# Three quarters of an MLP's down projection as seven block products instead of eight

## The chip, the cores and the metric

The kernel runs on one core of one Trainium2 chip, as one program. The metric is device time in microseconds, the median of several runs. The traces are single executions taken by the hardware profiler.

## The reference

Two post-norm residual layers over x of 512 tokens by 1024 features, in float32. Each layer has a token mixer (mLSTM in layer 0, causal pooling in layer 1), a four-head cross attention into 256 memory tokens whose keys and values both layers share, and an MLP. After each of the three, x becomes LayerNorm(alpha * x + sublayer(x)). The part that changes is the second product of this:

```python
def sq_relu_mlp(x, w1, b1, w2, b2):
    return jnp.square(jax.nn.relu(x @ w1 + b1)) @ w2 + b2
```

with w1 of 1024 x 4096 and w2 of 4096 x 1024 in each layer. Of the rest it matters that `mem_k` and `mem_v` are computed once and read by `memory_cross_attn` in layer 0 and again in layer 1.

## The kernel before

Each float32 operand of a large product is split into a high part h (rounded for TensorE's float32r) and a low part l, the remainder. `mm3` (L167) makes one tile product of three matmuls: h by h, h by l, l by h (L168, L169, L170). A weight unit of 128 x 1024 is loaded into `raw`, cast to `wh` by ScalarE (L131) and turned into `wl = raw - wh` by VectorE (L132); there are three `raw` buffers and five each of `wh` and `wl`, shared by all weights of the program.

The MLP goes by four quarters q of the 4096 hidden features (L733). In each, the **up** part makes eight tiles of 128 hidden features by 512 tokens (`feat_tile`, 24 matmuls of 512 columns each); `evh` (L711) turns a tile into the hi and lo parts of relu squared with two operations on ScalarE and two on VectorE. The **down** part (L721) goes by two halves of 512 output columns: four weight units, then for each of four groups of 128 tokens eight `mm3` into one PSUM bank (24 matmuls of 512 columns), and VectorE adds the bank onto x (L726). A down part is 2 x 4 x 24 = 192 matmuls. In layer 0 the last quarter also sets up and runs the pooling mixer of layer 1 (`pool_setup`, L560), by halves of the tokens, with up tiles of 256 columns. The keys and values of the memory lie in eight tiles of the pool `vkv` from before layer 0's attention until layer 1's attention.

The code names tiles and a scheduler decides the order: each engine gets one fixed list of instructions and works through it from the first to the last, and an instruction waits for semaphores of the other engines. All loads are issued by SyncE (SP) into one queue, in the order of its list. So an instruction that waits holds up everything behind it on its engine.

The lines that the prediction uses:

```python
        h = wh_p.tile([P, WU], F32R, tag="wh", name=f"wh{n}")
        l = wl_p.tile([P, WU], F32R, tag="wl", name=f"wl{n}")
        A.copy(h, r)
        V.tensor_tensor(l, r, f32(h), ALU.subtract)
```

```python
                ps = token_proj(f"m{n}{hf}{t}", hid, w, t)
                V.tensor_tensor(x[t][:, hs], x[t][:, hs], ps, ALU.add)
```

Of the kernel before, what the change touches and what calls it, by code (L numbers as in the profile page):

```python
# [15 lines left out]
P = 128  # L16
# [5 lines left out]
H = 4  # L22
# [19 lines left out]
def trunk(ctx: ExitStack, tc: tile.TileContext, a: dict, out: bass.AP):  # L42
# [29 lines left out]
    class Act:  # L72
        """hi and lo parts of a feature-major array [1024, S], in two halves of 512 features"""
# [15 lines left out]
    def t5(name, dt=F32):  # L89
        return t5_p.tile([P, 1280], dt, tag="t5", name=name)  # L90

    def t2(name, n=512, dt=F32):
        return t2_p.tile([P, 512], dt, tag="t2", name=name)[:, :n]

    class ActT:
        """hi and lo parts of a feature-major array [1024, S], in two halves of 256 tokens"""
# [161 lines left out]
    def feat_first(name, n, srcs, x, evac):  # L258
        """The first n tiles of 128 features, the first half of the tokens ahead of the second"""
# [38 lines left out]
    for q in range(4):  # L298
        r = vkv_p.tile([P, 2, 516], F32, tag="vkv", name=f"xr{q}")[:, :, :S]
# [40 lines left out]
    def scores(h):  # L340
        """(k q^T) * exp(log weights) of head h, hi and lo, by tiles of keys"""
# [33 lines left out]
    # v: token-major, with a column of ones for the denominator  # L375
    vh = [vkv_p.tile([P, NT, 258], F32R, tag="vkv", name=f"vh{h}") for h in range(H)]
    vl = [vkv_p.tile([P, NT, 258], F32R, tag="vkv", name=f"vl{h}") for h in range(H)]
# [74 lines left out]
    # o gate  # L452
# [51 lines left out]
    def mem_k(n):  # L504
        """K^T of heads 2n, 2n + 1"""
        t = [vkv_p.tile([P, 1032], F32R, tag="vkv", name=f"k{n}{p}")[:, :1024] for p in "hl"]
# [8 lines left out]
    def mem_v():  # L515
        for mt in range(2):
            mv.append([vkv_p.tile([P, 1032], F32R, tag="vkv", name=f"v{mt}{p}")[:, :1024] for p in "hl"])
# [101 lines left out]
    for i in range(DEPTH):  # L619
        # cross attention  # L620
# [112 lines left out]
        for q in range(4):  # L733
# [17 lines left out]
            first = 0  # L751
            if q == 0:
                feat_first(f"h{n}", 4, lambda m: a["w1"][i, m], xm, lambda c, ps: evh(hid.k(c), c, q, ps, n))
                first = 4
                assert not later
                b2 = t5(f"b2{i}")[:, :D]
                ld(b2, a["b2"][i : i + 1, :].broadcast_to([P, D]))
                for t in range(NT):
                    V.scalar_tensor_tensor(x[t], x[t], ALPHA, b2, ALU.mult, ALU.add)
            for m in range(first, KC):  # L760
                evh(hid.k(m), m, q, feat_tile(f"h{n}{m}", a["w1"][i, 8 * q + m], xm, aux_p, "aux"), n)
            for hf in range(2):
                for t in down(hid, q, hf, range(NT), n):
                    for z in range(2):
                        ld(out[tok(t), hf_cols(z)], x[t][:, hf_cols(z)])


def _layout(inp):
    c = np.ascontiguousarray

    def feat(w):
        """[D, n * 128] -> [n, 128 (of a k tile), k tile, 128]"""
# [3 lines left out]
    def half(w):  # L776
        """[D, n * 512] -> [n, 4, 128, 2 k tiles * 512]"""
# [69 lines left out]
```

## Time and profile before

| | |
|---|---|
| runs | 1244.35, 1247.54, 1248.63 us, median 1247.54 |
| span of the profiled execution | 1242.4 us |
| TensorE busy | 1231.8 us (99%), 6457 matmuls |
| VectorE busy | 711.6 us (57%) |
| ScalarE busy | 503.8 us (41%) |
| DMA | 139.85 MB, mean 113 GB/s |

The page gives no time for the profiled execution but its span; the median of the runs is 5.1 us above it. A busy share is an average over the whole span, so a stage has to be read by itself. A matmul's record is longer than its turn on the engine, since matmuls are pipelined: the distance from one start to the next is what one costs.

### The profile page before, as it was taken

Reading aid. Unit: us, or ns where it says so; the run is one execution under the profiler, and the core shown is the slowest. Engines: PE = TensorE matmul, PEld = TensorE weight load, DVE = VectorE, ACT = ScalarE, POOL = GpSimd, SP = SyncE. Lnnn points to the kernel's source line nnn. Section 1 sums busy time; section 2 is a strip of 40 time slices with the busy share of each in tenths; the row PEclk is TensorE's granted clock in tenths of the full one; section 3 lists DMA queues with packets and bytes.
Section 4 is the critical chain, followed back from the end, with each engine's and each line's share of the span. In section 5 each row is a group of like instructions: output and inputs, shape, how many; then the busy total and the mean of one; then the engine's idle time right before and its main releaser. Section 6 shows DMA issues by size and latency. Waiting matters only on the chain.

```text
span 1242.4 us, 16082 instructions
## 1 busy us (share of the span) xinstructions
PE 1231.8 (99%) x6457; PEld 1053.7 (85%) x6457; DVE 711.6 (57%) x1062; ACT 503.8 (41%) x773; POOL 8.5 (1%) x34
## 2 busy tenths in 40 slices
PE   9999999999999999999999999999999999999997
PEld 6877889889889888888889899998988888888886
DVE  6775466485559534425356889775853442534446
ACT  7576675334423513314235454552351331422420
POOL 0000000000000000000000000000000000000000
PEclk9999999999999999999999999999999999999999
DMA  6232346333323423323336545532332332422411
GB/s 236 64 102 85 103 137 217 119 107 106 98 85 90 131 85 102 102 68 120 118 109 196 169 131 161 170 100 68 103 119 85 107 97 68 131 73 88 133 51 68
DMA packets 41786, 139.85 MB, mean 113 GB/s; under 512 B 5068, under 2 KB 5324, under 8 KB 41712
## 3 DMA queue, kind: packets, MB, share of 16 engines
q1 hardware_dynamic: 41712, 138.84, 35.5%
q8 instruction: 50, 0.82, 0.3%
q14 instruction: 24, 0.20, 0.0%
HBM read 136.72 MB, written 2.10 MB: 112 GB/s over the span
## 4 chain that ended last, share of the span: by engine, by line
PE 94%; DVE 3%; DMA 2%; issue 1%; ACT 0%; SPq 0%; DVEq 0%; ACTq 0%
PE h L169 9%; PE h L168 9%; PE h L170 9%; PE m L170 9%; PE m L168 9%; PE m L169 9%; PE ao L169 2%; PE ao L170 2%; PE ao L168 2%; PE q L169 2%; PE q L170 2%; PE q L168 2%; PE v L168 1%; PE qk L170 1%; PE qk L168 1%; PE v L170 1%
## 5 line engine op out<-in xcount | busy, mean ns | idle before, releaser
L131 ACT CAST wh<-raw 128x1024 fp32r<-128x1024 f32 x232 | 244.3, 1055 | 540.3 <-PE m L170 217.0
L132 DVE TENSOR_TENSOR wl<-raw,wh 128x1024 fp32r<-128x1024 f32 x232 | 283.8, 1224 | 262.7 <-ACT wh L131 257.3
L726 DVE TENSOR_TENSOR xp<-xp,m 128x512 f32<-128x512 f32 x32 | 22.0, 686 | 82.3 <-PE m L170 82.3
L726 DVE TENSOR_TENSOR xin<-xin,m 128x512 f32<-128x512 f32 x32 | 21.9, 686 | 65.9 <-PE m L170 65.9
L168 PE MATMUL h<-xm01h,wh 128*128 128x256 f32 (+1 forms) x176 | 59.0, 335 | 0.0
L168 PE MATMUL h<-xm00h,wh 128*128 128x256 f32 (+1 forms) x176 | 58.5, 333 | 0.0
L170 PE MATMUL h<-xm00h,wl 128*128 128x256 f32 (+1 forms) x176 | 58.4, 332 | 0.0
L170 PE MATMUL h<-xm01h,wl 128*128 128x256 f32 (+1 forms) x176 | 58.3, 331 | 0.0
L169 PE MATMUL h<-xm00l,wh 128*128 128x256 f32 (+1 forms) x176 | 58.3, 331 | 0.0
L169 PE MATMUL h<-xm01l,wh 128*128 128x256 f32 (+1 forms) x176 | 58.3, 331 | 0.0
L168 PE MATMUL h<-xm10h,wh 128*128 128x512 f32 (+1 forms) x144 | 52.8, 367 | 0.0
L168 PE MATMUL h<-xm11h,wh 128*128 128x512 f32 (+1 forms) x144 | 52.8, 367 | 0.0
L169 PE MATMUL h<-xm10l,wh 128*128 128x512 f32 (+1 forms) x144 | 52.6, 366 | 0.0
L170 PE MATMUL h<-xm11h,wl 128*128 128x512 f32 (+1 forms) x144 | 52.6, 365 | 0.0
L170 PE MATMUL h<-xm10h,wl 128*128 128x512 f32 (+1 forms) x144 | 52.6, 365 | 0.0
L169 PE MATMUL h<-xm11l,wh 128*128 128x512 f32 (+1 forms) x144 | 52.6, 365 | 0.0
L714 ACT ACTIVATE r<-h,b 128x512 f32<-128x512 f32 (+1 forms) x72 | 45.6, 634 | 0.3 <-PE h L170 0.2
L716 DVE TENSOR_TENSOR s<-r 128x512 f32<-128x512 f32 (+1 forms) x72 | 45.0, 625 | 0.0
L169 PEld LDWEIGHTS h<-xm00l,wh 128*128 128x128 f32 x176 | 33.4, 190 | 3.2
L168 PEld LDWEIGHTS h<-xm00h,wh 128*128 128x128 f32 x176 | 33.4, 190 | 3.2
L170 PEld LDWEIGHTS h<-xm01h,wl 128*128 128x128 f32 x176 | 33.4, 190 | 3.2
L168 PEld LDWEIGHTS h<-xm01h,wh 128*128 128x128 f32 x176 | 33.4, 190 | 3.1
(594 smaller groups left out, 3268.4 us busy)
## 6 DMA issues: line engine op xcount, KB each, us to landing
raw<-in_w SPq DMA_DIRECT2D x144, 512.0 KB, 3.7
raw<-in_w_q SPq DMA_DIRECT2D x24, 512.0 KB, 4.4
raw<-in_w_ao SPq DMA_DIRECT2D x16, 512.0 KB, 3.7
raw<-in_w_qk SPq DMA_DIRECT2D x8, 512.0 KB, 4.5
raw<-in_w_v SPq DMA_DIRECT2D x8, 512.0 KB, 4.7
raw<-in_w_o SPq DMA_DIRECT2D x8, 512.0 KB, 4.2
raw<-in_w_k SPq DMA_DIRECT2D x8, 512.0 KB, 3.9
raw<-in_w_kvv SPq DMA_DIRECT2D x8, 512.0 KB, 4.7
```

The costliest lines, as they stand in the source:

```text
L131: A.copy(h, r)
L132: V.tensor_tensor(l, r, f32(h), ALU.subtract)
L168: T.matmul(out_, l[0], r[0], start=start, stop=False)
L169: T.matmul(out_, l[0], r[1], start=False, stop=False)
L170: T.matmul(out_, l[1], r[0], start=False, stop=stop)
L714: A.activation(r, ps, AF.Relu, bias=b1[:, i, 8 * q + c : 8 * q + c + 1], scale=1.0)
L716: V.tensor_tensor(s, r, r, ALU.mult)
L726: V.tensor_tensor(x[t][:, hs], x[t][:, hs], ps, ALU.add)
```

## The change

In the first three quarters of each layer's MLP, the down part takes the 512 tokens x 1024 hidden features as 2 x 2 blocks A11, A12, A21, A22 and the quarter of w2 as B11 to B22, and makes their product from seven block products. `product` (new) is one of them: two PSUM banks, each of four `mm3`, so 24 matmuls of 512 columns. The squared hidden tiles stay in float32 (`s`), and VectorE makes the sums of blocks; each of the seven left operands is split into hi and lo by a cast of 1024 columns on ScalarE and a subtraction of 1024 columns on VectorE (`split`), each of the seven right operands by two of each (`weight_split`), and the sums of weights are eight more additions of 1024 columns (`each`). Four products are gathered in SBUF over the quarters (`into`: a copy by ScalarE in the first quarter, an addition by VectorE in the others), three are added to x at once (`onto`), and after the third quarter `gather` adds the four gathered sums to x in sixteen operations of 512 columns.

The new tiles need room: the pools `vkv`, `t5` and `t2` become a scope that is closed while the three quarters run and opened again for the fourth. So the keys and values are written to DRAM during layer 0 and read back before the fourth quarter.

```diff
+        if i == 0:
+            kv_flat = [z for w in mk + mv for z in w]
+            spill = dram_p.tile([len(kv_flat), P, 1024], F32, name="spill")
+            for n, z in enumerate(kv_flat):
+                ld(spill[n], f32(z))
...
+        enter(hid=12, rawd=6, t2=2)
...
+        def product(name, lhs, rhs, evac):
+
+            for g in range(2):
+                ps = acc_p.tile([P, 512], F32, tag="acc", name=f"{name}{g}")
+                for k in range(4):
+                    w = rhs[k // 2]
+                    mm3(ps, tuple(z[:, k, tok(g)] for z in lhs), (w[0][:, k % 2], w[1][:, k % 2]), start=k == 0, stop=k == 3)
+                evac(g, ps)
...
+                A.activation(r, ps, AF.Relu, bias=b1[:, i, 8 * q + m : 8 * q + m + 1], scale=1.0)
+                A.activation(s[m // 4][:, m % 4], r, AF.Square)
...
+                if m == 3 or m == first == 4:
+                    L["M1"] = split(f"a11{n}", a11)
+                    V.tensor_tensor(a11, a11, a21, ALU.subtract)
+                    L["M7"] = split(f"q3{n}", a11)
+            V.tensor_tensor(a21, a21, a22, ALU.subtract)
+            L["M5"] = split(f"q1{n}", a21)
+            V.scalar_tensor_tensor(a11, a11, -1.0, a22, ALU.mult, ALU.subtract)
+            L["M6"] = split(f"q2{n}", a11)
+            L["M2"] = split(f"a12{n}", a12)
+            V.tensor_tensor(a12, a12, a11, ALU.add)
+            L["P3"] = split(f"q4{n}", a12)
+            L["P4"] = split(f"a22{n}", a22)
...
+            b11 = load("b11", 0, 0)
+            product(f"m1{n}", L["M1"], weight_split(f"b11{n}", b11), into("M1"))
+            b12, b22 = load("b12", 1, 0), load("b22", 1, 2)
+            each(b11, b11, b12, ALU.add)
+            each(b12, b12, b22, ALU.add)
+            product(f"m7{n}", L["M7"], weight_split(f"t3{n}", b12), into("M7"))
+            product(f"m5{n}", L["M5"], weight_split(f"t1{n}", b11), into("M5"))
+            each(b11, b11, b22, ALU.add)
+            product(f"m6{n}", L["M6"], weight_split(f"t2{n}", b11), into("M6"))
+            product(f"p3{n}", L["P3"], weight_split(f"b22{n}", b22), onto(0, 1))
+            b21 = load("b21", 0, 2)
+            product(f"m2{n}", L["M2"], weight_split(f"b21{n}", b21), onto(0, 0))
+            each(b11, b11, b21, ALU.add)
+            product(f"p4{n}", L["P4"], weight_split(f"t4{n}", b11), onto(1, 0))
...
+                V.tensor_tensor(u, u, m7, ALU.add)
+                V.tensor_tensor(x21, x21, u, ALU.add)
...
+        for q in range(3):
+            up_down(q, f"{i}{q}")
+        gather()
+        enter(**mixing)
+        if i == 0:
...
+            for n, z in enumerate(kv_flat):
+                ld(f32(z), spill[n])
```

On TensorE's list a down part now holds 7 x 24 = 168 matmuls, in the order M1, M7, M5, M6, P3, M2, P4. Three places of the other lists matter; a name is the program's, with the layer and the quarter at its end (`t201l0`: low part of the first unit of the sum of weights t2, layer 0, quarter 1).

**Place 1: VectorE (DVE) from the last up tile of layer 0's second quarter into its down part.** Before:

```order
L719 TENSOR_TENSOR h011l_4371<-s017_4516,h011h_4370 128x512
L726 TENSOR_TENSOR xin0_2110<-xin0_2110,m0100_4544 128x512
L726 TENSOR_TENSOR xin1_2112<-xin1_2112,m0101_4570 128x512
L726 TENSOR_TENSOR xin2_2114<-xin2_2114,m0102_4596 128x512
L132 TENSOR_TENSOR wl93_4657<-raw93_4654,wh93_4656 128x1024
L132 TENSOR_TENSOR wl94_4663<-raw94_4660,wh94_4662 128x1024
L132 TENSOR_TENSOR wl95_4669<-raw95_4666,wh95_4668 128x1024
L726 TENSOR_TENSOR xin3_2116<-xin3_2116,m0103_4622 128x512
```

Now, from the last row that needs that up tile's buffer, in two pieces that follow each other:

```order
L772 TENSOR_TENSOR t101l0_4666<-b11010_4577,t101h0_4665 128x1024
L832 TENSOR_TENSOR s010_4271<-s010_4271,s011_4272 128x4x256
L834 SCALAR_TENSOR_TENSOR s010_4271<-s010_4271,s011_4272 128x4x256
L846 TENSOR_TENSOR sum0a_3825<-sum0a_3825,m1010_4589 128x512
L763 TENSOR_TENSOR q101l_4556<-s010_4271,q101h_4555 128x1024
L846 TENSOR_TENSOR sum0a_3825<-sum0a_3825,m1011_4603 128x512
L763 TENSOR_TENSOR q201l_4561<-s010_4271,q201h_4560 128x1024
L763 TENSOR_TENSOR a1201l_4565<-s011_4272,a1201h_4564 128x1024
L846 TENSOR_TENSOR sum0b_3826<-sum0b_3826,m7010_4637 128x512
L837 TENSOR_TENSOR s011_4272<-s011_4272,s010_4271 128x4x256
L772 TENSOR_TENSOR t101l1_4670<-b11011_4578,t101h1_4669 128x1024
L846 TENSOR_TENSOR sum0b_3826<-sum0b_3826,m7011_4651 128x512
```

```order
L763 TENSOR_TENSOR q401l_4570<-s011_4272,q401h_4569 128x1024
L763 TENSOR_TENSOR a2201l_4574<-s011_4272,a2201h_4573 128x1024
L846 TENSOR_TENSOR sum0b_3826<-sum0b_3826,m5010_4673 128x512
L824 TENSOR_TENSOR b11010_4577<-b11010_4577,b22010_4621 128x1024
L846 TENSOR_TENSOR sum0b_3826<-sum0b_3826,m5011_4687 128x512
L824 TENSOR_TENSOR b11011_4578<-b11011_4578,b22011_4622 128x1024
L772 TENSOR_TENSOR t201l0_4704<-b11010_4577,t201h0_4703 128x1024
L772 TENSOR_TENSOR t201l1_4708<-b11011_4578,t201h1_4707 128x1024
```

Before, VectorE made one weight unit's low part here and there and added finished banks to x. Now the operands of M5, M6, P3, M2 and P4 are made in this stretch, and the low part of M6's first weight unit (`t201l0`) stands 19th, behind six additions of finished banks (L846).

**Place 2: VectorE at the end of layer 0's third quarter.** Before:

```order
L726 TENSOR_TENSOR xin2_2114<-xin2_2114,m0212_5280 128x512
L132 TENSOR_TENSOR wl113_5409<-raw113_5406,wh113_5408 128x1024
L132 TENSOR_TENSOR wl114_5446<-raw114_5443,wh114_5445 128x1024
L132 TENSOR_TENSOR wl115_5483<-raw115_5480,wh115_5482 128x1024
L726 TENSOR_TENSOR xin3_2116<-xin3_2116,m0213_5306 128x512
L132 TENSOR_TENSOR wl116_5520<-raw116_5517,wh116_5519 128x1024
L716 TENSOR_TENSOR s0300_5402<-r0300_5400 128x256
```

Now:

```order
L881 TENSOR_TENSOR sum0a_3825<-sum0a_3825,sum0b_3826 128x512
L853 TENSOR_TENSOR xin2_2116<-xin2_2116,p4020_5407 128x512
L884 TENSOR_TENSOR xin2_2116<-xin2_2116,sum0a_3825 128x512
L882 TENSOR_TENSOR xin2_2116<-xin2_2116,sum0a_3825 128x512
L878 TENSOR_TENSOR sum0a_3825<-sum0a_3825 128x512
L883 TENSOR_TENSOR xin3_2118<-xin3_2118,sum0b_3826 128x512
L853 TENSOR_TENSOR xin3_2118<-xin3_2118,p4021_5421 128x512
L880 TENSOR_TENSOR xin1_2114<-xin1_2114,sum0a_3825 128x512
L151 TENSOR_TENSOR wl88_5519<-raw88_5516,wh88_5518 128x1024
```

The low part of the first weight unit of the fourth quarter (`wl88`) stands behind the addition of the last bank (`p4021`) and behind most of `gather`; before, the units of the second to fourth up tile (`wl113` to `wl115`) stood ahead of the last bank, and the first one further up still.

**Place 3: SyncE's loads from there on.** Before:

```order
L65 DMA b101_5362<-in_ln_b 128x512
L65 DMA wpr0_5340<-in_w_pool 128x1024 [waits DMAHW1_49,DVE_49]
L65 DMA wpr1_5348<-in_w_pool 128x1024 [waits DMAHW2_49,DVE_49]
L65 DMA raw112_5369<-in_w1 128x1024 [waits DMAHW4_49,DVE_49]
L65 DMA raw113_5406<-in_w1 128x1024 [waits DMAHW3_49,DMAHW0_49,DVE_49]
L65 DMA raw114_5443<-in_w1 128x1024 [waits DMAHW1_49,DVE_49]
L65 DMA raw115_5480<-in_w1 128x1024 [waits DMAHW5_49,DMAHW2_49,DVE_49]
```

Now:

```order
L84 DMA kv0_5463<-spill_3524 128x1024 [waits DMAHW1_49,PE_49]
L84 DMA kv1_5464<-spill_3524 128x1024 [waits DMAHW2_49]
L84 DMA kv2_5465<-spill_3524 128x1024
L84 DMA kv3_5466<-spill_3524 128x1024
L84 DMA kv4_5467<-spill_3524 128x1024 [waits DMAHW5_49]
L84 DMA kv5_5468<-spill_3524 128x1024 [waits DMAHW6_49]
L84 DMA kv6_5469<-spill_3524 128x1024 [waits DMAHW7_49]
L84 DMA kv7_5470<-spill_3524 128x1024 [waits DMAHW0_49]
L84 DMA band_5483<-in_band 128x1152 [waits DMAHW1_49]
L84 DMA psc_5485<-in_pool_scale 128x1024 [waits DMAHW2_49]
L84 DMA raw89_5553<-in_w1 128x1024 [waits DMAHW3_49,DVE_49]
L84 DMA raw90_5590<-in_w1 128x1024 [waits DMAHW4_49,DVE_49]
```

The first load of the eight keys and values waits for TensorE: it overwrites operands of the products. Behind it stand the other seven, the pooling band and scale, and then the weights of the second up tile (`raw89`), which before stood among loads that wait only for a free `raw` buffer.

## Rows read from the trace of the kernel before

**Rows 1.** Page, part 1 and part 4: busy shares, and the chain that ended last.
```profile
PE 1231.8 (99%) x6457; PEld 1053.7 (85%) x6457; DVE 711.6 (57%) x1062; ACT 503.8 (41%) x773; POOL 8.5 (1%) x34
PE 94%; DVE 3%; DMA 2%; issue 1%; ACT 0%; SPq 0%; DVEq 0%; ACTq 0%
```
**Rows 2.** Busy time by stretch: a down part, then an up part, of layer 0.
```profile
core 0: us, PE busy (x) PEld busy (x) DVE busy (x) ACT busy (x) POOL busy (x), PEclk, DMA share, GB/s
434.00:478.00 44.00, 44.00 (x196) 36.44 (x195) 15.02 (x17) 9.68 (x10) 0.00 (x0) 1.00 0.20 66
478.00:521.00 43.00, 43.00 (x192) 35.59 (x191) 20.27 (x24) 16.98 (x22) 0.00 (x0) 1.00 0.40 130
```
**Rows 3.** Waits of all engines: who waited for whom, total us, times, longest us.
```profile
DVE wl L132 <- ACT wh L131: 257.3, 131, 10.3
ACT wh L131 <- PE m L170: 217.0, 49, 15.6
ACT wh L131 <- PE h L169: 168.4, 64, 4.7
```
**Rows 4.** Timeline of TensorE: matmuls twelve apart, 512 columns, then 256 (start, us).
```profile
521.17 0.39 PE L168 MATMUL m<-wh,h010h 128*128 128x512 f32 x1
...
523.89 0.39 PE L168 MATMUL m<-wh,h011h 128*128 128x512 f32 x1
...
722.43 0.28 PE L168 MATMUL h<-xm00h,wh 128*128 128x256 f32 x1
...
723.87 0.28 PE L168 MATMUL h<-xm01h,wh 128*128 128x256 f32 x1
```
**Rows 5.** Groups by line and form: VectorE and ScalarE operations (busy us, mean ns).
```profile
L132 DVE TENSOR_TENSOR wl<-raw,wh 128x1024 fp32r<-128x1024 f32 x232 | 283.8, 1224 | 262.7 <-ACT wh L131 257.3
L759 DVE SCALAR_TENSOR_TENSOR xin<-xin,b 128x1024 f32<-128x1024 f32 x4 | 4.8, 1219 | 0.0
L726 DVE TENSOR_TENSOR xin<-xin,m 128x512 f32<-128x512 f32 x32 | 21.9, 686 | 65.9 <-PE m L170 65.9
L716 DVE TENSOR_TENSOR s<-r 128x512 f32<-128x512 f32 x56 | 38.3, 685 | 0.0
L131 ACT CAST wh<-raw 128x1024 fp32r<-128x1024 f32 x232 | 244.3, 1055 | 540.3 <-PE m L170 217.0 <-PE h L169 168.4 <-PE ao L170 36.2
```
**Rows 6.** DMA issues: KB each, median us from issue to landing.
```profile
raw<-in_w SPq DMA_DIRECT2D x144, 512.0 KB, 3.7
band<-in_band SPq DMA_DIRECT2D x1, 576.0 KB, 5.4
psc<-in_pool_scale SPq DMA_DIRECT2D x1, 512.0 KB, 3.6
```
**Rows 7.** Busy time by stretch: start, memory keys and values, layer 0's fourth quarter.
```profile
10.00:15.00 5.00, 5.00 (x23) 3.85 (x22) 2.97 (x5) 3.21 (x6) 0.32 (x3) 1.00 1.04 412
15.00:20.00 5.00, 5.00 (x23) 4.14 (x23) 4.49 (x6) 4.03 (x6) 0.00 (x0) 1.00 0.98 387
200.00:250.00 50.00, 50.00 (x230) 41.74 (x229) 26.30 (x29) 17.04 (x20) 0.00 (x0) 1.00 0.53 175
660.00:665.00 5.00, 5.00 (x44) 5.00 (x43) 3.22 (x6) 3.48 (x6) 0.00 (x0) 1.00 0.73 231
```
**Rows 8.** TensorE's start: timeline, and the busy row of its first stretch.
```profile
1.31 4.21 PE L282 MATMUL warm<-zero 128*128 128x512 f32 x9 [1.31 <-POOL zero L279]
...
9.74 0.40 PE L168 MATMUL qk<-x00h,wh 128*128 128x512 f32 x1
9.98 0.39 PE L169 MATMUL qk<-x00l,wh 128*128 128x512 f32 x1
...
1.00:5.00 4.00, 3.69 (x9) 2.92 (x10) 0.80 (x2) 2.07 (x3) 1.86 (x10) 1.00 0.79 220
```

More of the change, by code (lines that the diff above doesn't have):

```diff
@@ L1 @@
-from contextlib import ExitStack
+from contextlib import ExitStack, contextmanager
 import numpy as np
@@ L62, in trunk, with scope, enter @@
     aux_p = pool("aux", 2, space=bass.MemoryType.PSUM)
+    scoped = {}
+    @contextmanager
+    def scope(**bufs):
+        with ExitStack() as st:
+            for name, n in bufs.items():
+                scoped[name] = st.enter_context(tc.tile_pool(name=name, bufs=n))
+            yield
+        for name in bufs:
+            del scoped[name]
+    scopes = ExitStack()
+    def enter(**bufs):
+        scopes.close()
+        scopes.enter_context(scope(**bufs))
+    mixing = dict(vkv=8, t5=6, t2=7)
+    enter(**mixing)
     def ld(dst, src):
@@ L298, in trunk @@
     for q in range(4):
[L299 removed]
+        r = scoped["vkv"].tile([P, 2, 516], F32, tag="vkv", name=f"xr{q}")[:, :, :S]
         for z in range(2):
@@ L504, in mem_k @@
     def mem_k(n):
-        t = [vkv_p.tile([P, 1032], F32R, tag="vkv", name=f"k{n}{p}")[:, :1024] for p in "hl"]
+        t = [scoped["vkv"].tile([P, 1032], F32R, tag="vkv", name=f"k{n}{p}")[:, :1024] for p in "hl"]
         for c in range(4):
@@ L731, in down, with split, weight_split @@
                         yield t
-        for q in range(4):
+        def split(name, src):
+            h, l = [scoped["hid"].tile([P, 4, 256], F32R, tag="hid", name=f"{name}{p}") for p in "hl"]
+            A.copy(h, src)
+            V.tensor_tensor(l, src, f32(h), ALU.subtract)
+            return h, l
+        def weight_split(name, src):
+            us = []
+            for j, r in enumerate(src):
+                h = wh_p.tile([P, WU], F32R, tag="wh", name=f"{name}h{j}")
+                l = wl_p.tile([P, WU], F32R, tag="wl", name=f"{name}l{j}")
+                A.copy(h, r)
+                V.tensor_tensor(l, r, f32(h), ALU.subtract)
+                us.append([z.rearrange("p (k m) -> p k m", m=512) for z in (h, l)])
+            return us
@@ new lines, in gather @@
+        def gather():
+            for g in range(2):
+                u, w, f, m7 = (sums[z][:, g] for z in ("M1", "M6", "M5", "M7"))
+                x11, x12, x21, x22 = (x[2 * r + g][:, hf_cols(c)] for r in range(2) for c in range(2))
+                V.tensor_tensor(x11, x11, u, ALU.add)
+                V.tensor_tensor(u, u, w, ALU.add)
+                V.tensor_tensor(x12, x12, f, ALU.add)
+                V.tensor_tensor(x12, x12, u, ALU.subtract)
+                V.tensor_tensor(u, u, m7, ALU.add)
+                V.tensor_tensor(x21, x21, u, ALU.add)
+                V.tensor_tensor(x22, x22, f, ALU.add)
+                V.tensor_tensor(x22, x22, u, ALU.subtract)
@@ L734, in trunk @@
+        for q in range(3):
+            up_down(q, f"{i}{q}")
+        gather()
+        enter(**mixing)
+        if i == 0:
+            kv_flat = [scoped["vkv"].tile([P, 1032], F32R, tag="vkv", name=f"kv{n}")[:, :1024] for n in range(len(kv_flat))]
+            for n, z in enumerate(kv_flat):
+                ld(f32(z), spill[n])
+            mk[:] = [kv_flat[0:2], kv_flat[2:4]]
+            mv[:] = [kv_flat[4:6], kv_flat[6:8]]
+        for q in range(3, 4):
             n = f"{i}{q}"
@@ L750, in trunk @@
             hid = Act(f"h{n}")
[L751 to L760, printed above, removed]
+            for m in range(KC):
                 evh(hid.k(m), m, q, feat_tile(f"h{n}{m}", a["w1"][i, 8 * q + m], xm, aux_p, "aux"), n)
```

62 lines of the change are left out of this document (52 added, 10 removed).

## The prediction, made before the change was run

> **What bounds the kernel now.** I read the shares first, then the chain, then one stage by itself, then the waits. TensorE is busy 99% of the span and 94% of the chain that ended last is TensorE [rows 1]. In a down part of 44 us TensorE is busy throughout while VectorE works 15.0 us and ScalarE 9.7; in an up part of 43 us VectorE works 20.3 and ScalarE 17.0 [rows 2]. The waits say the same from the other side: the longest are the helpers' waits for TensorE, 217.0 and 168.4 us for a free `wh` buffer, and VectorE's wait of 257.3 us for ScalarE's cast behind them [rows 3]. What one matmul costs is read from starts: twelve of 512 columns take 523.89 - 521.17 = 2.72 us, so 0.2267 each, and twelve of 256 columns 1.44, so 0.12 each [rows 4]. Matmuls taken away here shorten the run, for as long as the helpers stay ahead.
>
> **What is removed.** A down part has 192 matmuls, now 168: 24 x 0.2267 = 5.44 us less. Three quarters in two layers: 6 x 5.44 = **-32.6 us**.
>
> **What the helpers get.** Before, VectorE's work per quarter was 15.0 + 20.3 = 35 us in 87 [rows 2]. Now it makes low parts of 8 up units, 14 units for the products and 7 left operands, 8 sums of weights and 4 of hidden blocks: 41 operations of 1024 columns. The nearest rows are 1.224 us (two operands) and 1.219 (scalar form) [rows 5]; I take 1.22, 50 us. With the banks, 14 x 0.686 from the second quarter on, it is 60 of 82 us. On average that fits. But the operands of the last five products need the last up tile, so I walk VectorE's list there (place 1). Time 0 is the end of the block's last up tile.
>
> *Second and third quarter of each layer (four blocks).* The first row, `t101l0`, waits for a cast that needs the buffer of the up tile just finished: 1.06 us [rows 5], so VectorE starts at 1.1. Up to `t201l0` stand 13 operations of 1.22 and 6 of 0.69: 1.1 + 15.9 + 4.1 = 21.1. TensorE has M1, M7 and M5 before M6: 72 x 0.2267 = 16.3 us. M6's second matmul needs `t201l0`; until 21.1 only two matmuls of M6 (0.45 us) can run. About 0.6 of the loss comes early, since M5's eighth matmul needs `t101l1` (8 wide and 3 narrow rows: 1.1 + 9.8 + 2.1 = 13.0, against 10.9 + 1.6 = 12.5). Lost: 21.1 - 16.3 - 0.45 = 4.4, with semaphores between 4.4 and 4.6. Later operands are in time: t4's second low part is VectorE's 32nd row at about 35, and P4 starts at 16.3 + 4.5 + 16.3 = 37.1. So **4 x 4.5 = +18.0 us**. Bounds: 3.5 to 5.5 each, a row of the walk more or less.
>
> *First quarter of each layer (two blocks).* ScalarE copies the four gathered products there, so the six narrow rows are gone, and `t200l0` is the 11th wide one: 1.1 + 13.4 = 14.5, before 16.3. Nothing lost.
>
> *The fourth quarter of layer 0 (places 2 and 3).* The first load of keys and values waits for TensorE; what it overwrites is read by the last product, so it is issued when that ends (call it T). Behind it in the queue: eight loads of 0.524 MB, the band 0.59, the scale and `raw89` 0.524 each, 5.83 MB. Full DMA moved 412 and 387 GB/s [rows 7]; at 390 that is 14.9 us. A single load lands 3.7 us after issue [rows 6], 2.4 more than its own 1.3 of data, so `raw89` lands at T + 17.3 to 17.8. ScalarE first casts a pooling weight, then `raw89` (2 x 1.06): the second up tile starts at T + 20. `raw90` needs a `raw` buffer that the pooling weights hold until VectorE has scaled them (scale at T + 16.4, then four operations of 0.69 and a split): issued at T + 20.5, landed T + 24.6, cast and low part done at T + 26.9. With tiles of 24 x 0.12 = 2.9 us TensorE would be at that matmul at T + 6.0. **+21 us.** The wait for `wl88` at the first tile (next paragraph) is inside this. Bounds: 14 us, if loads behind the reload land at the best rate and the pooling weights don't hold the buffer, to 31, at the 231 GB/s of the old fourth quarter [rows 7]. I take 21: when requests queue up, the full-rate rows are nearest.
>
> *The fourth quarter of layer 1.* No reload, but `gather` stands on VectorE's list as in place 2. At T the list has about five narrow rows and the split to do, 5 x 0.69 + 1.22 = 4.7 us; four matmuls run meanwhile. **+4.4 us**, bounds 2.5 to 5.4.
>
> *Without cost.* The spill: SyncE's list has its eight stores among the loads for the memory's values and the mixer's output projection, where DMA was 0.53 busy and TensorE never idle [rows 7]. 4.19 MB take 10.8 us of a full queue, which the other 0.47 of 50 us covers; without that cover up to 10.8 us would be lost there, since the stores wait for the finished keys and values with weights behind them. ScalarE: 29 casts of 1.06 per quarter, 31 us of 82, beside its squares; in the walk its casts stand ready before VectorE comes to their low parts.
>
> *The clock.* [...] The start is nearest: the first nine matmuls took 4.21 us, 0.47 each and twice 0.2267, though the column reads 1.00 there too, and 0.23 was reached at 9.74, 8.4 us after the first [rows 8]. So after a stop between 0 and 8.4 us may run at half speed, a loss of 0 to 4.2 us per stop. [...] I take 2 us, half a stop, for layer 1's fourth quarter, where TensorE is all but idle for over 4 us. In layer 0's fourth quarter half speed hides behind `raw90`.
>
> Sum: -32.6 + 18.0 + 21 + 4.4 + 2 = **+12.8 us**. Against the profiled execution, 1242.4 becomes 1255.2; the median of the runs lies 5.1 above that span, so 1260.3, rounded to **1260**.
>
> **Rivals.**
>
> *A. The half clock follows the waits at M6 too.* Place: M6 and P3 in four blocks, TensorE idle there for two gaps of some 2 us with two matmuls between. For: the start [rows 8]. Against: the gaps are short. Price: 4 x 2.1 to 4.2 = 8 to 17, so 1268 to 1277.
>
> *B. The reload is slower.* At 231 GB/s [rows 7] `raw89` lands 10 us later: 1270. For: the old fourth quarter never got above that. Against: it was not asking for more.
>
> *C. The reload does not hold up the weights (the other side).* Place: the fourth quarter of layer 0. If the memory under the keys and values is free several products earlier, the eight loads go out while TensorE still works, and only the 4.4 us of `gather` remain: -16.6, so 1243.7, just faster. It decides from about 15 us of lead on. Against: the list shows the first load waiting for TensorE alone among compute engines, and the pools reopen only behind the last product.
>
> *D. VectorE keeps up.* If `t201l0` were done by 15.3 in the walk, a us ahead of M6, all four M6 waits would go: 1260 - 18 = 1242, also just faster. That needs (15.3 - 1.1 - 4.1) / 13 = 0.78 us for a wide operation, and the rows of that width stand at 1.224 and 1.219 [rows 5].
>
> **Chances.** Forecast 0.60, A 0.18, B 0.10, C 0.06, D 0.03, others 0.03. The forecast's own range is 1252 to 1268: 4 us from the four M6 waits, and as much from the reload and the unseen clock. The range to hold eight in ten takes in the lower part of A and B and reaches a little below: 1250 to 1275. A difference of 0.3%, 3.7 us, is about what a measurement can tell from none: faster (below 1243.8) 0.05, the same 0.08, slower (above 1251.3) 0.87.
>
> **What would show it.** Right: matmuls of products 0.2267 apart, 168 in a down part; in the second and third quarters TensorE idle for 4 to 5 us around M6's first matmuls, waiting for `t2` low parts on VectorE, and none in the first; TensorE idle for about 12 us after the first up tile of layer 0's fourth quarter, ended by ScalarE's cast of `raw89`, with DMA full; about 4 us lost at layer 1's first tile. Wrong: starts 0.45 apart after these waits (A); kv loads issued before the last product ends (C); no wait at M6 (D). If TensorE's idle time in all is below 25 us, the forecast fails.

## The result, and the profile after

The changed kernel takes **1261.01 us** (median of four runs, 1258.63 to 1261.73); the kernel before took 1246.74 beside it (four runs, 1244.35 to 1248.63). The ratio is 1.011, 95% interval 1.0094 to 1.0126: slower by 1.1%. The forecast was 1260, with a range of 1250 to 1275. The profiled execution is the run of 1258.63; its span is 1256.8 us, 14.4 above the span before, where the sum said 12.8.

First the page of the changed kernel: busy shares, TensorE's granted clock in 40 slices, and the chain, which answer to [rows 1].

```profile
PE 1217.9 (97%) x6313; PEld 1033.5 (82%) x6313; DVE 849.1 (68%) x1168; ACT 586.5 (47%) x867; POOL 8.5 (1%) x34
...
PEclk9999999999999999999987999999999999999999
...
PE 90%; DVE 4%; DMA 3%; ACT 1%; issue 1%; SPq 0%; DVEq 0%; ACTq 0%
```

There are 144 matmuls fewer, and TensorE is no longer busy throughout: 1256.8 - 1217.9 = 38.9 us without work, where [rows 1] left 10.6. TensorE's own waits say where:

```profile
PE h L187 <- ACT wh L150: 12.6, 1, 12.6
PE h L189 <- DVE wl L151: 4.9, 3, 2.5
...
PE m L188 <- DVE t201l L772: 1.4, 1, 1.4
...
PE m L187 <- ACT t201h L771: 0.9, 1, 0.9
```

The first row is the second up tile of layer 0's fourth quarter, the second the low part behind `gather`. The last two stand for four pairs alike, the waits at M6 in the second and third quarters of both layers (`t201`, `t202`, `t211`, `t212`).

The best way to see what a wait costs is from the start of one part to the start of the next. The table holds these for the kernel before, the one after, and the experiments below (us; the quarters count from 1, two numbers are layer 0 and layer 1). The last column runs from the start of layer 0's first down part to the end, since that part starts anywhere from 433.9 to 437.7 in these traces, whatever the edit.

| kernel | down 1 | down 2 | down 3 | up 4, layer 0 | up 4, layer 1 | down 1 to the end |
|---|---|---|---|---|---|---|
| before | 43.52, 43.52 | 43.53, 43.52 | 43.52, 43.52 | 23.03 | 43.52 | 808.3 |
| after | 39.36, 39.36 | 43.54, 43.68 | 42.21, 42.20 | 43.76 | 47.23 | 822.7 |
| e1_align | 39.04, 39.03 | 43.40, 43.43 | 41.90, 41.90 | 43.26 | 47.25 | 821.4 |
| e2_reload | 39.35, 39.36 | 43.61, 43.50 | 42.17, 42.18 | 34.43 | 45.66 | 811.2 |
| e3_left | 39.35, 39.35 | 39.35, 39.35 | 39.36, 39.35 | 43.09 | 50.25 | 811.7 |
| e4_gather | 39.35, 39.36 | 42.21, 43.74 | 42.20, 42.20 | 41.37 | 43.56 | 814.7 |
| e6_match | 38.08, 38.08 | 42.66, 42.72 | 41.16, 41.13 | 43.00 | 45.75 | 814.6 |
| c1 | 39.36, 39.35 | 39.35, 39.35 | 39.35, 39.36 | 28.92 | 43.55 | 796.0 |
| c6 | 39.36, 39.36 | 40.54, 40.55 | 43.98, 42.73 | 25.27 | 43.52 | 807.5 |
| c7 | 38.08, 38.08 | 38.08, 38.08 | 38.08, 38.08 | 29.50 | 43.52 | 790.1 |
| d2 | 38.08, 38.08 | 38.08, 38.08 | 38.08, 38.08 | 33.33 | 43.52 | 786.2 |

Before to after, the six down parts give -4.16 x 2 + 0.01 + 0.16 - 1.31 - 1.32 = -10.8 us, the two fourth up parts +20.7 and +3.7, and the rest of layer 0's fourth quarter, up to the attention, +0.8: 14.4 in all, the difference of the spans.

**The spacing was not forecast.** The timeline of TensorE in layer 0's first down part, twelve matmuls apart:

```profile
434.14 0.39 PE L187 MATMUL m<-b1100h,a1100h 128*128 128x512 f32 x1
...
436.95 0.40 PE L187 MATMUL m<-b1100h,a1100h 128*128 128x512 f32 x1
...
439.76 0.40 PE L187 MATMUL m<-t300h,q300h 128*128 128x512 f32 x1
```

Twelve take 2.81 us, 0.2342 each, against 0.2267 for the same shape in [rows 4]. Nothing waits there: 168 x 0.2343 = 39.36, the whole down part. So a down part saved 4.16 us where 5.44 was counted.

**M6.** The timeline of TensorE around the first weights of M6, in the second and then the third quarter of layer 0:

```profile
533.69 0.40 PE L189 MATMUL m<-t101h,q101l 128*128 128x512 f32 x1
534.98 0.73 PE L187 MATMUL m<-t201h,q201h 128*128 128x512 f32 x2 [0.90 <-ACT t201h L771]
537.13 0.80 PE L188 MATMUL m<-t201l,q201h 128*128 128x512 f32 x1 [1.42 <-DVE t201l L772]
...
538.58 0.63 PE L188 MATMUL m<-t201l,q201h 128*128 128x512 f32 x1
539.01 0.63 PE L189 MATMUL m<-t201h,q201l 128*128 128x512 f32 x1
```
```profile
624.22 0.51 PE L188 MATMUL m<-t202l,q202h 128*128 128x512 f32 x1 [1.42 <-DVE t202l L772]
624.57 0.39 PE L189 MATMUL m<-t202h,q202l 128*128 128x512 f32 x1
624.80 0.40 PE L187 MATMUL m<-t202h,q202h 128*128 128x512 f32 x1
```

The two waits cost 2.85 us (42.21 - 39.36). In the second quarters of both layers the matmuls behind them start 0.427 us apart (in layer 0 until 539.86), at a granted clock of 0.50: another 1.3 to 1.5 us. In the third quarters the same waits are followed by full speed (0.234 apart, granted clock 1.00). It isn't the place that decides this: in e4_gather below, whose edit comes after the third quarter, layer 0's second quarter has the same two waits and full speed behind them (0.23 apart, 42.21 in the table):

```profile
538.79 0.51 PE L188 MATMUL m<-t201l,q201h 128*128 128x512 f32 x1 [1.42 <-DVE t201l L772]
539.14 0.39 PE L189 MATMUL m<-t201h,q201l 128*128 128x512 f32 x1
539.37 0.40 PE L187 MATMUL m<-t201h,q201h 128*128 128x512 f32 x1
```

So a difference of 1.3 to 1.6 us at one such place, between two executions, can be the clock alone.

**Layer 0's fourth quarter.** SyncE's list, then busy time by stretch:

```profile
646.54 3.70 SPq L84 DMA_DIRECT2D kv<-spill  x8
650.29 1.09 SPq L84 DMA_DIRECT2D band<-in_band  x1
651.42 0.47 SPq L84 DMA_DIRECT2D psc<-in_pool_scale  x1
653.73 14.22 SPq L84 DMA_DIRECT2D raw<-in_w  x3
```
```profile
646.00:650.00 4.00, 1.52 (x9) 1.23 (x8) 3.96 (x7) 0.00 (x0) 0.00 (x0) 0.92 0.60 216
650.00:655.00 5.00, 3.61 (x20) 3.41 (x19) 1.84 (x4) 0.89 (x2) 0.00 (x0) 0.72 1.02 393
655.00:660.00 5.00, 0.00 (x0) 0.00 (x0) 0.11 (x1) 0.00 (x0) 0.00 (x0) 0.62 1.02 418
660.00:665.00 5.00, 0.00 (x0) 0.00 (x0) 2.17 (x4) 0.84 (x1) 0.00 (x0) 0.50 0.46 182
665.00:670.00 5.00, 3.15 (x13) 2.85 (x14) 3.73 (x4) 2.10 (x3) 0.00 (x0) 0.50 0.48 145
```

The last product's last matmul starts at 646.12 and the reload is issued at 646.54; DMA then moves 393 and 418 GB/s, near the 412 and 387 of [rows 7], and TensorE stands still from 653.6 to 666.20. The clock column falls to 0.50 and stays there for TensorE's first matmuls after the stop. Most of the first tile, behind its wait of 2.48 us for `wl88`, ran at 0.50 too: from 649.51 to 652.71 the matmuls of 256 columns start 0.213 us apart, where [rows 4] have 0.12.

### The profile page after: what moved, and what is told of

The parts are those of the page before. It is cut to its first block, busy times and chain, and to the rows that moved or that the text cites. A ratio compares the mean times of both kernels' runs of the same rounds, so it can differ in the third digit from the quotient of the medians.

```text
span 1256.8 us, 15934 instructions
## 1 busy us (share of the span) xinstructions
PE 1217.9 (97%) x6313; PEld 1033.5 (82%) x6313; DVE 849.1 (68%) x1168; ACT 586.5 (47%) x867; POOL 8.5 (1%) x34
## 4 chain that ended last, share of the span: by engine, by line
PE 90%; DVE 4%; DMA 3%; ACT 1%; issue 1%; SPq 0%; DVEq 0%; ACTq 0%
PE h L189 9%; PE h L188 9%; PE h L187 9%; PE m L188 7%; PE m L189 6%; PE m L187 6%; PE ao L189 2%; PE ao L187 2%; PE ao L188 2%; PE q L188 2%; PE q L189 2%; PE q L187 2%; PE p L189 2%; PE p L188 2%; PE p L187 2%; DMA raw<-in_w 1%
## 5 line engine op out<-in xcount | busy, mean ns | idle before, releaser
L151 DVE TENSOR_TENSOR wl<-raw,wh 128x1024 fp32r<-128x1024 f32 x184 | 224.7, 1223 | 182.4 <-ACT wh L150 180.3
L150 ACT CAST wh<-raw 128x1024 fp32r<-128x1024 f32 x184 | 193.0, 1051 | 296.5 <-PE h L188 79.5
L187 PE MATMUL h<-xm00h,wh 128*128 128x256 f32 (+1 forms) x176 | 59.8, 340 | 12.6 <-ACT wh L150 12.6
L824 DVE TENSOR_TENSOR b<-b,b 128x1024 f32<-128x1024 f32 x48 | 58.4, 1220 | 0.4
L187 PEld LDWEIGHTS h<-xm00h,wh 128*128 128x128 f32 x176 | 34.6, 196 | 16.1 <-ACT wh L150 12.8
L189 PEld LDWEIGHTS h<-xm00h,wl 128*128 128x128 f32 x176 | 34.5, 196 | 6.8 <-DVE wl L151 3.6
L188 PEld LDWEIGHTS h<-xm01l,wh 128*128 128x128 f32 x176 | 34.3, 195 | 3.1
L189 PEld LDWEIGHTS h<-xm10h,wl 128*128 128x128 f32 x144 | 27.6, 192 | 6.8 <-DVE wl L151 2.2
```

Source lines behind the costliest of these rows:

```text
L187: T.matmul(out_, l[0], r[0], start=start, stop=False)
L188: T.matmul(out_, l[0], r[1], start=False, stop=False)
L189: T.matmul(out_, l[1], r[0], start=False, stop=stop)
L824: V.tensor_tensor(d, u, v, op)
```

## The experiments

The theory: the time came from four separate places (spacing, M6, reload, `gather`). The rivals are named with each run. Every ratio is against the kernel before, on the same chip.

**e1_align: is it the 32-byte offset of the tiles?**

```diff
     st_p = pool("st", 3)
+    pool("pad", 1).tile([P, 8], F32, name="pad")
```

> One 32-byte tile is added behind the pool st, so that the pools opened after it begin at a multiple of 64 bytes in each partition instead of 32 bytes past one; nothing else changes. Theory (address): the products' matmuls are 0.2343 us apart because their stationary tiles begin 32 bytes off; now they are 0.2267 apart, a down part of the first quarter takes 168 x 0.2267 = 38.1 us in place of 39.36, and since VectorE is no faster, M6 waits some 0.55 us longer in the other four: 2 x 1.3 + 4 x 0.7 = 5.5 us less in all, span about 1251 (1248 to 1253). Rival (shape or traffic: tiles of 4x256, or VectorE and ScalarE working beside the products): starts stay 0.234 apart, a down part of the first quarter stays at 39.4, span 1256 to 1258.

Measured: 1258.92 us, ratio 1.0108 (1.0092 to 1.0124), no different from the change. The first down parts took 39.04 us. The theory fell: of the 1.3 us by which a first down part is too long, 0.3 went.

**b_shift: the same question put to the kernel before.**

```diff
+    pool("pad", 1).tile([P, 8], F32, name="pad")
     act_p = pool("act", 8)
```

> The kernel before, with one 32-byte tile ahead of the pool act, so that nearly every stationary tile now begins 32 bytes past a multiple of 64; no other change. Theory (address): about 4,000 matmuls of 512 columns go from 0.2267 to 0.234 us apart, 4,000 x 0.0077 = 31 us more: span about 1273 (1268 to 1282, the upper end if matmuls of 256 columns pay too). Rival (shape or traffic): no change, span 1241 to 1245.

Measured: 1245.45 us, ratio 0.9995 (0.9985 to 1.0005). With every tile 32 bytes off nothing changes. The two runs together say that it isn't the offset of a tile by itself.

**e2_reload: is it the reload that holds the weights?**

```diff
-            for n, z in enumerate(kv_flat):
-                ld(f32(z), spill[n])
...
                         evh(hid.k(m, cs), m, q, feat_tile(f"h{n}{z}{m}", a["w1"][i, 8 * q + m], xm, acc_p, "acc", cs), f"{n}{z}")
+                        if m % 2:
+                            j = 4 * z + m // 2
+                            ld(f32(kv_flat[j]), spill[j])
```

> The eight reloads of keys and values are issued one after every second up tile of layer 0's fourth quarter, not all ahead of it. Theory (the reload holds the weights on the queue): of the 20.7 us that the fourth quarter's up tiles lost, the wait for the second tile's weights falls from 12.6 to some 3 us, and 10 to 14 us go in all: span 1243 to 1247; what is left there is gather ahead of the first low part and the pooling weights' two raw buffers. Rival 1 (the pooling mixer's weights hold the raw buffers and the band and the scale the queue, so the wait stays): 0 to 4 us less, span 1253 to 1257. Rival 2 (the bytes only move on: weights and reloads share the queue for longer and each tile waits a little): 4 to 8 us less.

Measured: 1249.83 us, ratio 1.004 (1.0025 to 1.0055); 11.5 us less from the first down part on, 9.3 of it in this up part and 1.6 in layer 1's fourth up part, which the edit doesn't touch: there the wait is the same, but full speed follows it (45.66 us for the part in place of 47.23). The waits of layer 0's up part, from TensorE's timeline:

```profile
651.29 0.40 PE L189 MATMUL h<-xm00h,wl 128*128 128x256 f32 x1 [2.48 <-DVE wl L151]
658.59 0.58 PE L187 MATMUL h<-xm00h,wh 128*128 128x256 f32 x1 [2.89 <-ACT wh L150]
660.37 0.58 PE L189 MATMUL h<-xm00h,wl 128*128 128x256 f32 x1 [0.99 <-DVE wl L151]
```

The wait of 12.6 us fell to 2.89, as the theory said; both rivals fell. The 2.48 ahead of it, behind `gather`, stayed as it was.

**e3_left: does M6 wait for its place in the list, or for the sum of VectorE's work?**

```diff
             L["M6"] = split(f"q2{n}", a11)
-            L["M2"] = split(f"a12{n}", a12)
-            V.tensor_tensor(a12, a12, a11, ALU.add)
-            L["P3"] = split(f"q4{n}", a12)
-            L["P4"] = split(f"a22{n}", a22)
...
             product(f"m6{n}", L["M6"], weight_split(f"t2{n}", b11), into("M6"))
+            L["M2"] = split(f"a12{n}", a12)
+            V.tensor_tensor(a12, a12, a11, ALU.add)
+            L["P3"] = split(f"q4{n}", a12)
+            L["P4"] = split(f"a22{n}", a22)
```

> The left operands of P3, M2 and P4 (four operations of 1024 columns on VectorE that stand ahead of M6's weights now) are written after M6, so VectorE comes to t2 some 4.9 us earlier. Theory (place in the list): the waits at M6 and the half clock behind two of them go, 14 us less, span about 1243. Rival (VectorE is behind by the sum of its work after the last up tile): the wait moves to P3 or P4, 1.5 to 3 us in each of the four blocks, and the first tile of both fourth quarters waits longer: span 1245 to 1253.

Measured: 1250.80 us, ratio 1.0044 (1.0028 to 1.006). All six down parts take 39.35 us, with no wait in any: inside the down parts the place in the list was all. But the work moved back is met at the fourth quarters, where TensorE's first low part is later than in the change (2.48 and 1.79):

```profile
648.35 0.58 PE L189 MATMUL h<-xm00h,wl 128*128 128x256 f32 x1 [5.49 <-DVE wl L151]
```
```profile
1153.26 0.50 PE L189 MATMUL h<-xm10h,wl 128*128 128x512 f32 x1 [4.80 <-DVE wl L151]
```

So the rival was right about one of its two places: 14.2 us gained in the down parts, 3.0 given back in layer 1.

**e4_gather: is the wait at the fourth quarter's first tile `gather`?** The call moves from ahead of the loop to behind its second up tile.

```diff
-        gather()
...
+                if m == 1:
+                    gather()
```

> The sixteen operations of gather are written after the second up tile of both fourth quarters and no longer ahead of the first. Theory (gather delays the first low part): the wait at layer 1's first up tile and the half clock behind it go, its up part falls from 47.2 to 43.5 or 44 us; in layer 0 nothing is gained, since the wait for the reload ends later than gather: 3 to 4.5 us less in all, span 1252 to 1254. Rival (VectorE is behind there from the products, not from gather; or the sixteen operations delay the third tile instead): up part of layer 1's fourth quarter 46 to 48 us, span 1256 to 1258.

Measured: 1253.11 us, ratio 1.0055 (1.0037 to 1.0073). Layer 1's up part fell to 43.56, as free as before, and layer 0's by 2.4 us, where nothing was expected. From the first down part on 8.0 us went; 1.3 of it is the clock in layer 0's second quarter, not the edit.

**b_high: the height of the address?** The kernel before, with `act` opened last.

```diff
-    act_p = pool("act", 8)
     wh_p = pool("wh", 5)
...
     st_p = pool("st", 3)
+    act_p = pool("act", 8)
```

> The kernel before with the pool act (which holds the left operands of the down parts, and the moving operands of the up parts) opened last, so that its tiles lie from byte 163,680 of each partition on and no longer from 4,352 on; the keys, values and weighted scores come down below 122,000. No instruction changes. In the changed kernel every matmul whose stationary tile lies at 151,136 or above takes 0.234 us, and those at 111,000 or below 0.2267. Theory (a high address of the stationary operand costs 0.007 us a matmul): a down part goes from 43.52 to about 45.0 us, 2,600 matmuls in all give +18 to +20, span about 1261; up parts stay at 43.5, and the products with the values fall to 0.227. If a high moving operand costs the same, up parts grow to 45.0 too and the span to about 1274. Rival (traffic of VectorE and ScalarE beside the products, or the 4x256 shape of the tiles): down parts stay at 43.5, span 1241 to 1245.

Measured: 1273.04 us, ratio 1.0215 (1.02 to 1.023). A program with the same instructions in the same order is 26 us slower. TensorE's timeline, twelve apart in a down part, then in an up part, then six apart in the products with the values:

```profile
533.91 0.39 PE L168 MATMUL m<-wh,h010h 128*128 128x512 f32 x1
...
536.72 0.40 PE L168 MATMUL m<-wh,h011h 128*128 128x512 f32 x1
```
```profile
491.91 0.40 PE L168 MATMUL h<-xm01h,wh 128*128 128x512 f32 x1
...
494.71 0.40 PE L168 MATMUL h<-xm00h,wh 128*128 128x512 f32 x1
```
```profile
331.57 0.40 PE L168 MATMUL ov<-pt00h,v0h 128*128 128x512 f32 x1
...
332.97 0.39 PE L168 MATMUL ov<-pt00h,v0h 128*128 128x512 f32 x1
```

Down 0.234, up 0.233: traffic and tile shape are out, since neither changed. But the last pair speaks against height too: values and weighted scores now lie low, and still go at 0.233. What sorts the matmuls of 512 columns in the seven traces at hand by then (the two of the start, e1_align, b_shift, e2_reload, b_high and c6) is the distance between two addresses. Where the moving operand begins a multiple of 512 bytes from the next matmul's stationary operand, the median is 0.227 us (18,987 matmuls, more than eight in ten within 0.226 to 0.227); at the other distances it is 0.230 to 0.234 (8,500). In the kernel before, `act`, `wh` and `wl` followed one another in multiples of 4,096 bytes; in b_high `act` lies 96 bytes past a multiple of 512 from the weights. In the changed kernel the `hid` pool opens behind `st` and lies 352 bytes past a multiple of 512 from the weights (384 in e1_align).

**e6_match: the distance, set right.**

```diff
+    st_p = pool("st", 3)
     act_p = pool("act", 8)
...
     lnp_p = pool("lnp", 1)
-    st_p = pool("st", 3)
```

> The changed kernel with the pool st opened ahead of act and no longer behind lnp. The left operands of the products stay at byte 151,136 and above; their distance from the weight tiles (the moving operands) is now a multiple of 512 bytes, where it was 352 past one. No instruction changes. Over the traces so far, 18,987 matmuls of 512 columns whose moving operand lies a multiple of 512 bytes from the next stationary one have a median of 0.227 us from start to start, and all 8,500 others 0.230 to 0.234, at high addresses and at low ones. Theory (distance): product matmuls 0.2267 apart, a down part of the first quarter 38.1 us and no longer 39.36, and in the other four M6 waits some 0.55 us longer: 2 x 1.3 + 4 x 0.7 = 5.5 us less, from the start of the first down part to the end 817 us in place of 822.7. Rival (height of the address): 0.234 stays, 822 to 823.

Measured: 1254.76 us (1250.3 to 1257.86), ratio 1.007 (1.0052 to 1.0087). The timeline, twelve apart:

```profile
433.88 0.39 PE L187 MATMUL m<-b1100h,a1100h 128*128 128x512 f32 x1
...
436.60 0.39 PE L187 MATMUL m<-b1100h,a1100h 128*128 128x512 f32 x1
```

2.72 us again, and 38.08 for a first down part as expected. Height is out: the products' left operands lie where they lay. The profiled execution is 8.0 us shorter from there to the end, where 5.5 were expected, but it is the fastest of the six, and two of its waits in the fourth quarters (first tiles of both layers) are followed by full speed where the change had half (45.75 us in place of 47.23 for layer 1's up part; mean granted clock 0.989 in place of 0.986). By the medians, each taken against the kernel before beside it, the loss fell from 14.3 to 8.9 us: 5.4 less, as expected.

**c1: three edits at once.** The edits of e2_reload and e3_left, `gather` behind the third up tile, and in layer 0 `pool_setup` behind the eighth.

```diff
-                mixer, xnew, xa = pool_setup()
...
+                        if z == 0 and m == 2:
+                            gather()
+                            hid.get(1)
+                        if z == 0 and m == 7:
+                            mixer, xnew, xa = pool_setup()
```

> Three edits at once: the left operands of P3, M2 and P4 after M6; the reloads spread over layer 0's fourth quarter; gather after the third up tile, and in layer 0 the pooling mixer's set-up after the eighth. Theory (the losses are separate and add up): down parts 39.4 us in all six blocks (-14.1), layer 0's fourth up part from 43.8 to 28 to 32 us, layer 1's from 47.2 to 43.5: span 1226 to 1233, below the kernel before. Rival (VectorE has no room in layer 0's fourth quarter, and what is moved off one place is waited for at the next): span 1236 to 1245.

Measured: **1235.09 us**, ratio 0.9916 (0.9899 to 0.9933), faster than the kernel before. The losses are separate and nearly add up: e2_reload, e3_left and e4_gather by themselves took off 11.5, 11.0 and 8.0 us from the first down part on, 30.5 in all with what the clock gave, and c1 took off 26.7. All six down parts and layer 1's up part are free of waits. In layer 0's fourth quarter a part stays: its up part has 28.92 us, 5.9 more than before the change, and the stretch from there to the attention 6.6 more.

**c6: GpSimd for what VectorE has too much of.** As c1, with `gather` on GpSimd behind the first up tile, and two low parts of each block.

```diff
-            L["M2"] = split(f"a12{n}", a12)
+            L["M2"] = split(f"a12{n}", a12, G)
...
-                V.tensor_tensor(x11, x11, u, ALU.add)
+                G.tensor_tensor(x11, x11, u, ALU.add)
```

> As c1, but GpSimd, idle so far, does the sixteen operations of gather (now after the first up tile) and the low parts of two left operands (for M2 and P4) in each block. Theory (GpSimd works beside VectorE): VectorE has 11 us less to do in each fourth quarter and 2.4 us less in each block, span 1217 to 1226. Rival (the two engines get in each other's way on SBUF, or GpSimd takes several us for one operation so that M2 or P4 waits for it): no better than c1, VectorE's operations of 1024 columns beside GpSimd's take clearly more than 1.22 us.

Measured: 1244.66 us, ratio 0.9987 (0.9977 to 0.9997), 9.6 us slower than c1. Groups of GpSimd, and the timeline of VectorE and GpSimd in layer 0's second quarter:

```profile
L763 POOL TENSOR_TENSOR a2210l<-s,a2210h 128x1024 fp32r<-128x1024 f32 x1 | 8.0, 7990 | 6.7 <-ACT a2210h L762 6.7
...
L763 POOL TENSOR_TENSOR a1200l<-s,a1200h 128x1024 fp32r<-128x1024 f32 x1 | 2.4, 2439 | 283.1 <-ACT a1200h L762 283.1
```
```profile
526.36 1.22 DVE L763 TENSOR_TENSOR q201l<-s,q201h 128x1024 fp32r<-128x1024 f32 x1
...
527.04 2.81 POOL L763 TENSOR_TENSOR a1201l<-s,a1201h 128x1024 fp32r<-128x1024 f32 x1 [64.35 <-ACT a1201h L762]
...
527.49 3.43 DVE L772 TENSOR_TENSOR t101l<-b,t101h 128x1024 fp32r<-128x1024 f32 x1
```

GpSimd takes 2.4 to 8.0 us for what VectorE does in 1.22, and VectorE's subtraction that starts beside it takes 3.43. Not every operation of VectorE beside GpSimd is slow, but all 29 of 1024 columns that took 1.6 to 3.4 us stood beside one of GpSimd's. The rival was right in its times; that the two engines meet on SBUF was the author's estimate, and no row shows where they meet. Layer 0's up part did gain (25.27, 3.6 less than c1), but the down parts lost 10.4 us and the stretch behind the up part 5.0.

**c7: c1 with e6_match's order of pools.** On top of c1:

```diff
+    st_p = pool("st", 3)
     act_p = pool("act", 8)
...
-    st_p = pool("st", 3)
```

> As c1, with the pool st ahead of act as in e6_match. Theory (distance): 1,008 x 0.0076 = 7.7 us less on TensorE, of which VectorE, which now has 38.1 us and not 39.4 for a block, gives back up to 1.6 us in each of four blocks as waits at P3: from the start of the first down part to the end 796.0 in c1, now 788 to 795. Rival (height): no change, 795 to 797.

Measured: **1228.20 us**, ratio 0.9855 (0.9841 to 0.987), and 790.1 us from the first down part on. All six down parts take 38.08 us = 168 x 0.2267; VectorE gave nothing back at P3.

**d2: `gather` in pieces.** As c7, with `gather` two operations at a time (four in layer 1), and `pool_setup` behind the fourth up tile and no longer the eighth. These are two edits, so the run doesn't tell what each is worth by itself.

```diff
                 V.tensor_tensor(x11, x11, u, ALU.add)
+                yield
                 V.tensor_tensor(u, u, w, ALU.add)
+                yield
...
+                            for _ in range(2 if m >= 0 else 0):
+                                next(steps, None)
...
+                        if z == 0 and m == 3:
+                            mixer, xnew, xa = pool_setup()
```

> As c7, with gather written as two operations behind each up tile of layer 0's fourth quarter (four behind each in layer 1) and the pooling mixer's set-up behind the fourth up tile and no longer the eighth. Theory (VectorE's work comes in one lump ahead of low parts): TensorE's one wait of 3.6 us there becomes several short ones, the pooling part is no longer late, 2 to 4 us less than c7. Rival (VectorE is full through that stretch whatever the order): the same as c7 within 1.5 us.

Measured: **1224.52 us**, ratio 0.9829 (0.9816 to 0.9841), 1.7% faster than the kernel before. Its page and its longest waits of TensorE:

```profile
PE 1203.6 (99%) x6313; PEld 1030.5 (84%) x6313; DVE 847.0 (69%) x1168; ACT 587.6 (48%) x867; POOL 8.4 (1%) x34
```
```profile
PE h L187 <- ACT wh L150: 4.4, 2, 2.4
PE h L189 <- DVE wl L151: 2.0, 2, 1.2
```

From the first down part to the end it is 22.1 us below the kernel before: the whole 32.6 of the removed matmuls, less 10.5, nearly all of it in layer 0's fourth up part (33.33 - 23.03 = 10.3). The up part grew from c7's 29.50 to 33.33 while the end came 3.9 us earlier: the pooling set-up is inside it now, and the stretch from there to the attention fell from 86.1 to 78.9 us, as before the change. What of those 10.3 us could still go wasn't tried.

## Why the prediction was right, step by step

The total was right to 1.6 us of span because errors of both signs met: the products' spacing cost 7.7 us that the sum didn't have, and the M6 waits 6.6 less than it had. That they nearly cancel is luck. The steps, in the prediction's order:

- **Bound.** Right: without waits, the time follows TensorE matmul by matmul (c7 and d2, 38.08 in every block).
- **Removed matmuls, -32.6.** The count was right, the term mis-sized: -25.0. The step "24 x 0.2267" left the other 168 at their old price; they cost 0.0076 more each, 7.7 us in all. e6_match (0.2267) and b_high (0.234) show the cause: the distance between operands, which a pool's place sets.
- **M6, +18.0.** Place, engine and list row were right, the size too big: four times 2.85, 11.4 us, and 2.8 more by the clock. What the 4.5 holds for semaphores, 0.1 us, was the author's estimate; no run shows it by itself. The walk came to 21.1 us for the end of `t201l0`, 20.1 were measured (537.13 - 517.06), and TensorE was 0.55 later at M6 by its spacing. M5, which was to lose 0.6 early, didn't wait. The walk took the length of VectorE's records for their turns, though operations overlap. VectorE's timeline in that stretch:

```profile
522.24 1.22 DVE L763 TENSOR_TENSOR q101l<-s,q101h 128x1024 fp32r<-128x1024 f32 x1
523.38 0.68 DVE L846 TENSOR_TENSOR sum0a<-sum0a,m 128x512 f32<-128x512 f32 x1
523.97 1.22 DVE L763 TENSOR_TENSOR q201l<-s,q201h 128x1024 fp32r<-128x1024 f32 x1
525.11 1.22 DVE L763 TENSOR_TENSOR a1201l<-s,a1201h 128x1024 fp32r<-128x1024 f32 x1
```

  From one start to the next a wide operation (1024 columns) takes 1.14 us and a narrow one (512) 0.59 to 0.60; by these turns the walk comes to 19.6. "First quarter: nothing lost" was right (39.36 with no wait).
- **The reload, +21.** Right: 20.7. The second tile was forecast for 20 us after the end of the last product and came at 666.20 - 646.35 = 19.9; the cast of `raw89` ended the wait, with DMA full until past 660 (busy share 1.00 to 1.03 from 650 to 662), and e2_reload took nearly all of it away by moving the loads alone. Ahead of that cast ScalarE had a pooling weight to cast, which waited for the pooling scale from the same queue, as the prediction had it. The low part of `raw90`, forecast for 26.9 us after the last product, was done at 26.0 (672.34); TensorE, at half speed (granted clock 0.50), came to it at 672.93, so it didn't wait there, and half speed cost some 0.6 more. Half speed hid behind `raw90` almost as forecast.
- **`gather`, +4.4, and the clock, +2.** Both smaller, and together 3.7. The 2 was an estimate, half of the 4.2 us that the prediction took from the start [rows 8]; no run shows that term as such, and what the runs showed in its place is 1.7 us here, 1.3 to 1.5 at M6 in the second quarters and nothing in the third. TensorE's timeline at layer 1's first tile:

```profile
1158.88 0.40 PE L188 MATMUL h<-xm10l,wh 128*128 128x512 f32 x1
1161.06 0.57 PE L189 MATMUL h<-xm10h,wl 128*128 128x512 f32 x1 [1.79 <-DVE wl L151]
1161.43 0.63 PE L187 MATMUL h<-xm10h,wh 128*128 128x512 f32 x1
1161.86 0.63 PE L188 MATMUL h<-xm10l,wh 128*128 128x512 f32 x1
```

  Behind four matmuls the stop costs 2.0 us (2.18 from start to start in place of 0.23), and the matmuls behind it, most of them 0.43 apart at a granted clock of 0.50, another 1.7. The prediction's own terms, 4.7 less four matmuls, give 3.8 and not 4.4, and VectorE was further on than the five rows counted: the low part was done 2.8 us after the last product. e4_gather removes all of it.
- **Without cost.** The spill took nothing that these two traces show: layer 0's first down part starts at 434.14 us, where it started at 434.13 before.
- **Rivals.** A came true in half of its places: half speed behind M6 in the second quarters only, 2.8 us in place of 8 to 17, and e4_gather shows that even there it needn't come. Half speed followed the long stop (granted clock 0.50 at 665 us) and some of the short ones, not all. B fell (393 and 418 GB/s), C fell (the reload was issued 0.4 us after the last product's last start), D fell (M6 did wait).

Of the list of signs, three came out otherwise. The matmuls of products were 0.2343 apart and not 0.2267, and that sat under the largest term; TensorE's idle time at M6 was 2.3 us (0.90 + 1.42) in place of 4 to 5; and starts 0.43 apart, the sign of A, were seen behind half of those waits.

## What to carry to other kernels

Count a removed matmul at its old price, but check what the rest will cost where their operands now lie: a pool opened at another place cost 7.7 us here and 26 in b_high, with no instruction changed. Averages hid the rest: VectorE, with 32% of its time free, set the time at M6 and behind `gather` by rows that stood too late in its list, and a DMA queue that moved 118 GB/s on average by loads that stood too early in it. Moving a handful of statements and one pool turned 1.1% slower into 1.7% faster. Walk a list by start-to-start times of neighbours, not by the length of records. Before a gain of one or two us is put down to an edit, look whether the clock behind an unchanged wait was the same in both traces.

## What the runs showed of the hardware that was not expected

- A matmul of 512 columns (float32 split as here) took 0.2267 us from start to start where moving and next stationary operand lie a multiple of 512 bytes apart, and 0.230 to 0.234 at the other distances seen (0.234 in the change, 352 bytes past one; 0.232 in e1_align, 384 past). Matmuls of 256 columns showed nothing of it: medians of 0.120 at a multiple of 512, 0.117 to 0.119 elsewhere. Why is open.
- After waits of the same length at M6 (0.90 and 1.42 us) TensorE went on at half speed (0.427 us apart, granted clock 0.50) in the change's second quarters and at full speed (0.234) in its third quarters and in layer 0's second quarter of e4_gather, at the same place of the program; no row here shows what decides it.
- GpSimd's subtraction of 1,024 columns took 2.4 to 8.0 us in c6, and operations of VectorE beside GpSimd's took up to 3.43 in place of 1.22.
